# First shift and scale on TensorE, an ordered head, four landing buffers and a spread rotation in a two-layer hybrid trunk

## The chip, the cores and the metric

One core of a Trainium2 chip runs the whole kernel. The metric is the device time of one execution in microseconds (us), as the median of several. Engines are called as in the profile: PE is TensorE, DVE is VectorE, ACT is ScalarE, POOL is GpSimd, and SP is SyncE, whose queue issues most of the DMAs.

## The reference

What must be computed is a stack of two layers over 512 tokens of width 1024, conditioned on one vector c. Each layer normalises x, scales and shifts it by values computed from c (adaLN), projects it once to all inputs of two mixers (a sparse attention with an index of top keys, and a chunked state-space scan), merges the mixers by gates and adds the result to x.

```python
def _layer(x, c, w_ada, b_ada, norm_g, w_in, ...):
    mod = jax.nn.silu(c) @ w_ada + b_ada
    shift, scale, gate = jnp.split(mod, 3, axis=-1)
    h = _rmsnorm(x, norm_g) * (1.0 + scale[:, None, :]) + shift[:, None, :]
    proj = h @ w_in
    (q, k, v, g_att, qi, ki, wi, z, xbc, dt_raw, gl_att, gl_ssd) = _split_cols(proj, IN_SIZES)
    q = _rope(q.reshape(B, L, N_ATT_HEADS, HEAD_DIM), cos[:, None, :], sin[:, None, :])
    ...
    merged = jax.nn.sigmoid(gl_att) * y_att + jax.nn.sigmoid(gl_ssd) * y_ssd
    return x + gate[:, None, :] * (merged @ w_out)
```

All is float32. The kernel splits each factor of a product into a high and a low part of a shorter format and sums three products: high by high, low by high and high by low.

## The kernel before, in words

**Layout.** x lies transposed in SBUF: 128 channels on the partitions, eight channel blocks (k = 0 to 7), 512 tokens along the free dimension. `hh` and `hl` (tiles H0 and H1; in the profile both are called H) hold the high and low part of the normalised, scaled and shifted input. The modulation (adaLN) comes in 24 blocks of 128 channels per layer: 0 to 7 shift, 8 to 15 scale, 16 to 23 gate. For a block, `ada_block` (L147) multiplies a 128x1024 piece of weights by `cb`, which is silu(c) repeated on all partitions, on VectorE and accumulates along the row (L149); ScalarE adds the bias (L152 for a scale, `gsc`; L154 for a shift, `mod`).

**The head.** TensorE repeats c on all partitions by two multiplications with one row (L130), and ScalarE takes silu of it (L295). The four pairs of blocks of x are squared, one block of a pair by ScalarE (L297), the other by VectorE (L298), and added (L299). TensorE sums them over the channels with a constant (L301), 256 tokens into each of two banks. From each half comes a reciprocal root (`rstd_from`, L263 and L265 on ScalarE, two correction steps L266 and L267 on VectorE). Before the first H, blocks 8 and 0 of the modulation are needed. `make_h` (L310) builds H: a product on VectorE (L312), the high part on ScalarE (L313), the low part on VectorE (L315). `chain` (L142) fixes VectorE's order in the head, `in_row` (L288) a part of ScalarE's.

**The token projection.** `tok_section` (L365) loops over k and, within it, over two groups of weights: K (468 columns, with the index keys, the step sizes and the value) and Q (512 columns), for four token blocks each. L379, L380 and L381 are the three products, per token block one after the other. The weights come through class `W`: `load` starts a DMA of 512 KB into one of `RAWB` = 3 landing buffers `raw` (L175, on SP's queue), `split` casts the high part on ScalarE (L194) and subtracts on VectorE (L195). Modulation blocks of later use stand in the same list and land in the same buffers; so a load waits until the step that reads the buffer's former content is done. `pre0` builds H for the next k and the next two modulation blocks beside it.

**The rotations.** `rope_k` rotates the four token blocks of K: products with cosine (L435) and sine (L437) from the bank, a sum (L439), casts on ScalarE (L451, L452), low parts by subtraction on VectorE (L454, L455), transposes on TensorE (L466). `rope_q` does the same for Q (low part L489, transposes L494) and is written out in full behind it. Then come the channel blocks: `block` (L249) with products L254, L255, L256, with other generators (index scores, state-space steps, attention) interleaved by `tick`.

**What sets the order.** The kernel's text gives a program order with priorities; a scheduler makes each engine's list from it, and the order of VectorE and ScalarE in the head is fixed by hand with dependencies that carry no wait. Loads stand in one list on SP's queue.

**Later.** In the attention, L798 and L799 make scores for four heads, L801 evicts them on VectorE with the row's maximum.

## Time and profile before

| | |
|---|---|
| time, median of 3 executions | 924.76 us (922.68 to 924.89) |
| profiled execution, its own time | 926.5 us |
| its span, first to last instruction | 924.7 us |
| mean granted TensorE clock | 0.992 |
| busy: PE, DVE, ACT, POOL | 906.5, 703.9, 521.0, 49.6 us |
| chain that ended last, share of the span | PE 88%, DVE 5%, DMA 4%, ACT 1% |
| moved by DMA | 128.05 MB, 138 GB/s |

Times are microseconds from the start of the span. The busy time of TensorE counts an instruction from its start to its modelled end, and instructions overlap, so a stretch can be full of busy time and yet run at the lower clock; the granted clock stands beside it, as a share of the full one. The chain is followed back from the last instruction to what released each step.

### The profile page before, as it was taken

The numbers are of one execution on the slowest core, as the hardware profiler recorded it, in microseconds if no ns is written. First come the engines' busy times: TensorE is split into PE (matmuls) and PEld (weight loads), VectorE is DVE, ScalarE is ACT, GpSimd is POOL, SyncE is SP. The second block draws the span as 40 slices with busy tenths as digits, with TensorE's granted clock in tenths as the row PEclk, the third lists the DMA queues.
The fourth block names the chain that finished last, engine by engine and source line by source line (L and its number), as shares of the span: only waits on it lengthen the run. The fifth ranks groups of instructions, "written<-read, shape, count | busy, mean of one in ns | idle before, by whom it ended". The sixth has DMA issues, their size and how long they took to land.

```text
span 924.7 us, 13016 instructions
## 1 busy us (share of the span) xinstructions
PE 906.5 (98%) x4780; PEld 743.8 (80%) x4780; DVE 703.9 (76%) x1384; ACT 521.0 (56%) x946; POOL 49.6 (5%) x53
## 2 busy tenths in 40 slices
PE   8999999999999999999999999999999999999996
PEld 4887788888887877777998878888888878778895
DVE  7987999999775765678497699999984675455834
ACT  5457894386265754535365588745653775463433
POOL 0000110031000000000000001102210000000000
PEclk8999999999999999999999999999999999999999
DMA  9832433232346432687344225234323532334502
GB/s 357 317 114 69 164 111 103 103 137 84 102 139 200 138 133 72 220 282 266 96 134 140 89 93 180 94 98 131 125 66 117 169 117 91 92 122 149 207 24 91
DMA packets 40609, 128.05 MB, mean 138 GB/s; under 512 B 4417, under 2 KB 6721, under 8 KB 40546
## 3 DMA queue, kind: packets, MB, share of 16 engines
q1 hardware_dynamic: 36162, 111.43, 36.6%
q0 software_dynamic: 4384, 15.80, 4.9%
q8 instruction: 37, 0.61, 0.3%
q14 instruction: 26, 0.21, 0.1%
HBM read 118.76 MB, written 8.46 MB: 138 GB/s over the span
## 4 chain that ended last, share of the span: by engine, by line
PE 88%; DVE 5%; DMA 4%; ACT 1%; issue 1%; SPq 0%; DVEq 0%; ACTq 0%
PE mm L254 21%; PE mm L255 21%; PE mm L256 21%; PE av L826 2%; PE tr L821 2%; DMA raw<-ada 2%; DVE wlo L195 1%; PE qk L723 1%; PE mm L379 1%; PE mm L381 1%; PE mm L380 1%; PE qk L798 1%; PE qk L799 1%; DMA raw<-wt 1%; PE av L740 1%
## 5 line engine op out<-in xcount | busy, mean ns | idle before, releaser
L254 PE MATMUL mm<-H,whi 128*128 128x512 f32 x640 | 258.6, 404 | 0.0
L256 PE MATMUL mm<-H,wlo 128*128 128x512 f32 x640 | 251.4, 393 | 0.0
L255 PE MATMUL mm<-H,whi 128*128 128x512 f32 x640 | 251.2, 393 | 0.0
L195 DVE TENSOR_TENSOR wlo<-raw,whi 128x1024 fp32r<-128x1024 f32 (+2 forms) x130 | 158.0, 1215 | 56.6 <-ACT whi L194 54.7
L194 ACT CAST whi<-raw 128x1024 fp32r<-128x1024 f32 (+2 forms) x130 | 130.3, 1003 | 113.1 <-PE mm L255 84.7
L254 PEld LDWEIGHTS mm<-H,whi 128*128 128x128 f32 x640 | 120.6, 188 | 26.3 <-issue 3.9
L256 PEld LDWEIGHTS mm<-H,wlo 128*128 128x128 f32 x640 | 120.5, 188 | 25.6 <-issue 0.3
L255 PEld LDWEIGHTS mm<-H,whi 128*128 128x128 f32 x640 | 120.7, 189 | 24.4 <-issue 1.9
L581 DVE MAX8 m<-B 128x8 f32<-128x256 f32 (+2 forms) x96 | 53.1, 554 | 1.2
L603 DVE SCALAR_TENSOR_TENSOR tmp<-mm,prm,tmp 128x511 f32<-128x511 f32 (+2 forms) x72 | 52.8, 736 | 0.0
L582 DVE MATCH_REPLACE8 B<-m,B 128x256 f32<-128x256 f32 (+2 forms) x96 | 52.0, 541 | 0.0
L254 PE MATMUL mm<-X,whi 128*128 128x512 f32 x128 | 51.6, 403 | 0.0
L256 PE MATMUL mm<-X,wlo 128*128 128x512 f32 x128 | 50.2, 392 | 0.3 <-DVE wlo L195 0.3
L803 ACT ACTIVATE S<-S,mx 128x128 f32<-128x128 f32 (+3 forms) x64 | 35.5, 556 | 25.3 <-DVE mx L801 25.2
L149 DVE SCALAR_TENSOR_TENSOR raw<-raw,KI 128x1024 f32<-128x1024 f32 x20 | 24.5, 1223 | 31.5 <-DMA raw<-ada 31.4
L712 ACT ACTIVATE X<-X,acs 128x128 f32<-128x128 f32 x128 | 40.5, 390 | 0.1
L255 PE MATMUL mm<-G,whi 128*128 128x512 f32 x96 | 37.7, 393 | 0.2 <-DVE G L870 0.2
L254 PE MATMUL mm<-S,A 128*128 128x256 f32 x128 | 36.9, 289 | 0.0
L256 PE MATMUL mm<-S,C 128*128 128x256 f32 x128 | 36.2, 283 | 0.0
L898 DVE SCALAR_TENSOR_TENSOR X<-mm,mod,X 128x256 f32<-128x256 f32 (+1 forms) x24 | 13.7, 571 | 28.5 <-PE mm L256 28.5
L822 ACT COPY B<-tr 128x512 f32<-128x512 f32 x40 | 22.7, 583 | 20.9 <-PE tr L821 20.6
L715 POOL TENSOR_TENSOR S<-S,G 128x768 f32<-128x768 f32 x16 | 31.1, 1954 | 60.8 <-ACT G L604 31.2
(269 smaller groups left out, 1766.0 us busy)
## 6 DMA issues: line engine op xcount, KB each, us to landing
raw<-wt SPq DMA_DIRECT2D x103, 512.0 KB, 3.5
raw<-ada SPq DMA_DIRECT2D x20, 512.0 KB, 3.9
X<-AD POOLq DMA_DIRECT2D x16, 512.0 KB, 4.4
raw<-wk SPq DMA_DIRECT2D x12, 468.0 KB, 3.4
B<-ada SPq DMA_DIRECT2D x9, 512.0 KB, 4.4
raw<-wq SPq DMA_DIRECT2D x8, 512.0 KB, 3.9
gsave<-tmp SPq DMA_DIRECT2D x16, 256.0 KB, 2.4
tmp<-gsave SPq DMA_DIRECT2D x16, 256.0 KB, 4.0
```

The source lines that it names most:

```text
L149: link(dve.scalar_tensor_tensor(w, w, 1.0, cb, op0=OP.mult, op1=OP.mult, accum_out=m))
L194: act.copy(hi[:, :n], r[:, :n])
L195: link(dve.tensor_sub(lo[:, :n], r[:, :n], raw(hi[:, :n])))
L254: pe.matmul(out, h, rh[:, k, cols], start=k == 0, stop=False)
L255: pe.matmul(out, h, rl[:, k, cols], start=False, stop=False)
L256: pe.matmul(out, lw, rh[:, k, cols], start=False, stop=k == n - 1)
L581: dve.max(m8, sc)
L582: dve.match_replace(sc, m8, sc, GONE)
L603: dve.scalar_tensor_tensor(cc[:, i:], p[:, :L - i], cw(3 - i), cc[:, i:], op0=OP.mult, op1=OP.add)
L712: act.activation(ab[:, h, i], ab[:, h, i], AF.Relu, scale=-1.0, bias=acs[:, 2 * kt + h, i:i + 1])
L715: pool.tensor_tensor(cs_, cs_, BC[:, 2 + g, 128:].rearrange("p (c l) -> p c l", c=3)[:, None] .to_broadcast([128, 2, 3, 128]), op=OP.mult)
L803: act.activation(PP[:, e, :n], PP[:, e, :n], AF.Exp, bias=mx[:, e:e + 1], scale=-1.0, accum_out=sums_[:, e:e + 1])
```

## The change

1. *First shift and scale on TensorE.* A new input `cc` is c as a 128x8 column tile, loaded on ScalarE's queue into `ccol`; silu of it is the first step on ScalarE. A new input `adn` holds blocks 8 and 0 of the first layer's modulation weights in the layout that TensorE takes as weights. Behind the sums stand 16 fp32 multiplications of a 128x128 weight tile and one column (L326 of the changed kernel), eight into each of two columns of one bank `rows`, then one idle multiplication of 512 columns (L331). ScalarE reads `rows`. The two L149 steps of VectorE for these blocks go.
2. *An ordered head.* Each Square stands before the Silu of the same turn. `rstd_from` is cut into `root` and `corrected`; ScalarE's order is now fixed through both roots, scale, first cast, shift, both halves of H, second cast. VectorE does the corrections and products of both halves first, then their low parts, then the split of the first weights. In `tok_section` all high-by-high and low-by-high products of a group come first, the four products with the low weights last; for the first k the order is fixed by dependencies.
3. *Four landing buffers* (`RAWB` = 4).
4. *Rotation of queries beside the channel blocks.* `rope_q` is spawned as a generator; the index waits until it is done and takes its tile `IX` only then.

```diff
-RAWB = 3
+RAWB = 4
...
+IDLE = 1
...
+    ccol = consts.tile([128, KT], F32, name="ccol")
+    act.dma_start(ccol, cc)
...
     def load_ada(k):
-        sp.dma_start(aws[2 * k + 1], ada[0, 8 + k])
-        sp.dma_start(aws[2 * k], ada[0, k])
+        sp.dma_start(aws[2 * k + 1], adn[1] if k == 0 else ada[0, 8 + k])
+        sp.dma_start(aws[2 * k], adn[0] if k == 0 else ada[0, k])
...
+        def cast(self, i, arow):
+            self.load(i)
+            n = self.src[i][1]
+            self.his[i] = wp.tile([128, 1024], F32R, name="whi", tag="whi", bufs=WB)
+            with tc.high_priority(W_PRIO):
+                arow(act.copy(self.his[i][:, :n], self.loaded[i][:, :n]))
...
+    in_row(act.activation(ccol, ccol, AF.Silu))
     for k in range(0, KT, 2):
+        sq, sq1 = scratch(), scratch()
+        in_row(act.activation(sq, xt[:, k], AF.Square))
         if k < 4:
             in_row(act.activation(*silu[k // 2], AF.Silu))
-        sq, sq1 = scratch(), scratch()
-        in_row(act.activation(sq, xt[:, k], AF.Square))
...
+    rows = bank("mm")
+    for b in (1, 0):
+        for k in range(KT):
+            made = pe.matmul(rows[:, b:b + 1], aws[b][:, k * 128:(k + 1) * 128], ccol[:, k:k + 1],
+                             start=k == 0, stop=k == KT - 1)
+            tc.add_manual_dep(made.ins, summed.ins.name, NOSYNC)
+            summed = made
+    for i in range(IDLE):
+        made = pe.matmul(warm.rearrange("p (a b) -> p a b", a=4), ones, ones[:, None, :].to_broadcast([128, 4, 128]),
+                         start=True, stop=True)
...
-    ada_block(0, 8, cb, aws[1], chain)
-    ada_block(0, 0, cb, aws[0], chain)
...
-                        pe.matmul(acc[t][:, :n], hh[:, k, ts], a, start=k == 0, stop=False)
-                        pe.matmul(acc[t][:, :n], hh[:, k, ts], b, start=False, stop=False)
-                        pe.matmul(acc[t][:, :n], hl[:, k, ts], a, start=False, stop=k == KT - 1)
+                        for h in (hh, hl):
+                            made = pe.matmul(acc[t][:, :n], h[:, k, ts], a, start=k == 0 and h is hh, stop=False)
...
+                    for t in blocks:
+                        pe.matmul(acc[t][:, :n], hh[:, k, t * 128:(t + 1) * 128], b, start=False, stop=k == KT - 1)
...
         def pre0(k):
             if k == 0:
-                for cols, s in zip(HALVES, sums):
-                    rstd_from(rst[:, cols], s, D, True, chain)
-                    h = make_h(0, k, cols, chain)
+                sides = [(rst[:, cols], s) for cols, s in zip(HALVES, sums)]
+                ts = [root(*side, in_row) for side in sides]
+                ada_block(0, 8, None, rows[:, 1:2], arow=in_row)
+                w.cast(ids0[0], in_row)
+                ada_block(0, 0, None, rows[:, 0:1], arow=in_row)
+                hs = [make_h(0, k, cols, chain, in_row) for cols in HALVES]
+                for side, t, h in zip(sides, ts, hs):
+                    corrected(*side, t, chain)
                     next(h)
-                    if cols.start == 0:
-                        w.split(ids0[0], chain)
-                        w.load(ids0[3])
+                w.cast(ids0[1], in_row)
+                for h in hs:
                     for _ in h:
                         pass
+                w.split(ids0[0], chain)
+                w.load(ids0[3])
...
-        for _ in rope_q():
-            pass
+        spawn(rope_q(), 1)
...
-        IX = slot("B2", [128, 1152], F32)
+        IX = []
...
         def index():
+            while any(g[0].__name__ == "rope_q" for g in gens):
+                yield "wait"
+            IX.append(slot("B2", [128, 1152], F32))
```

How the lists of the engines move is shown at three places. In them `H_163` and `H_180` are `hh`, `H_164` and `H_181` are `hl`; `mm`, `qk`, `tr` and `av` are banks of PSUM, where the sums lie in `av` and `tr`, the accumulators of K in `qk` and `mm`. Lines are those of each kernel.

ScalarE in the head, from the first reciprocal root; before:

```order
7 L263 ACTIVATE rst<-av,epst 128x256
8 L152 ACTIVATE gsc_116<-mod_114,gb_118,prm 128x1
9 L265 ACTIVATE tmp<-rst 128x256
10 L263 ACTIVATE rst<-tr,epst 128x256
11 L154 ACTIVATE mod_114<-mod_114,prm 128x1
12 L194 CAST whi<-raw 128x936
13 L265 ACTIVATE tmp<-rst 128x256
14 L313 ACTIVATE H_163<-tmp,mod_114 128x256
15 L194 CAST whi<-raw 128x1024
16 L313 ACTIVATE H_163<-tmp,mod_114 128x256
```

and in the changed kernel (L276 and L278 are the roots and squares, L158 the scale, L160 the shift, L190 and L209 casts, L344 the high part of H):

```order
10 L276 ACTIVATE rst<-av,epst 128x256
11 L278 ACTIVATE tmp<-rst 128x256
12 L276 ACTIVATE rst<-tr,epst 128x256
13 L278 ACTIVATE tmp<-rst 128x256
14 L158 ACTIVATE gsc_118<-mm,gb_120,prm 128x1
15 L190 CAST whi<-raw 128x936
16 L160 ACTIVATE mod_116<-mm,prm 128x1
17 L344 ACTIVATE H_180<-tmp,mod_116 128x256 x2
18 L190 CAST whi<-raw 128x1024
```

The scale, which stood behind the first root and read VectorE's sum (`mod`), now stands behind both roots and reads TensorE's bank; both halves of H stand before the second cast.

VectorE at the end of the token projection, where the accumulators of K are rotated, from the cosine product of token block 1; before (L435 cosine, L437 sine, L439 sum, L454 and L455 subtractions, L449 step sizes, L195 the split of channel weights):

```order
66 L435 TENSOR_TENSOR tmp<-qk,B_165 128x384
67 L454 TENSOR_TENSOR B_498<-tmp,B_498 128x4x64
68 L455 TENSOR_TENSOR B_498<-tmp,B_498 128x2x128
69 L437 TENSOR_TENSOR tmp<-qk,B_165 128x6x32 x2
70 L449 TENSOR_TENSOR dtr<-mm,prm 128x16
71 L439 TENSOR_TENSOR tmp<-tmp 128x384
72 L435 TENSOR_TENSOR tmp<-mm,B_165 128x384
73 L454 TENSOR_TENSOR B_498<-tmp,B_498 128x4x64
74 L437 TENSOR_TENSOR tmp<-mm,B_165 128x6x32 x2
75 L195 TENSOR_TENSOR wlo<-raw,whi 128x1024
76 L455 TENSOR_TENSOR B_498<-tmp,B_498 128x2x128
```

and in the changed kernel (L478, L480, L482, L497, L498, L492 and L210 are the same in that order):

```order
63 L478 TENSOR_TENSOR tmp<-qk,B_182 128x384
64 L497 TENSOR_TENSOR B_517<-tmp,B_517 128x4x64
65 L498 TENSOR_TENSOR B_517<-tmp,B_517 128x2x128
66 L480 TENSOR_TENSOR tmp<-qk,B_182 128x6x32 x2
67 L492 TENSOR_TENSOR dtr<-mm,prm 128x16
68 L482 TENSOR_TENSOR tmp<-tmp 128x384
69 L210 TENSOR_TENSOR wlo<-raw,whi 128x1024
70 L497 TENSOR_TENSOR B_517<-tmp,B_517 128x4x64
71 L498 TENSOR_TENSOR B_517<-tmp,B_517 128x2x128
72 L478 TENSOR_TENSOR tmp<-mm,B_182 128x384
73 L480 TENSOR_TENSOR tmp<-mm,B_182 128x6x32 x2
```

The split of the third channel weights, which stood behind the subtraction L454 of block 1 and the cosine and sine products of block 2, now stands ahead of all of them.

VectorE ahead of the first eviction of attention scores (L801, L846 in the changed kernel), where modulation blocks (L149, now L152) and splits (L195, now L210) are worked off; before:

```order
364 L149 SCALAR_TENSOR_TENSOR raw,mod_114<-raw,KI 128x1024
365 L195 TENSOR_TENSOR wlo<-raw,whi 128x1024
366 L764 SCALAR_TENSOR_TENSOR tmp<-C,prm,tmp 128x512 x3
367 L766 TENSOR_TENSOR D_2438<-tmp,X 128x512 x3
368 L195 TENSOR_TENSOR wlo<-raw,whi 128x1024
369 L764 SCALAR_TENSOR_TENSOR tmp<-C,prm,tmp 128x512
370 L149 SCALAR_TENSOR_TENSOR raw,mod_114<-raw,KI 128x1024
371 L766 TENSOR_TENSOR D_2438<-tmp,X 128x512
372 L195 TENSOR_TENSOR wlo<-raw,whi 128x1024
373 L149 SCALAR_TENSOR_TENSOR raw,mod_114<-raw,KI 128x1024
374 L801 ISA S,mx<-ctab,qk 128x128
```

and in the changed kernel:

```order
363 L210 TENSOR_TENSOR wlo<-raw,whi 128x1024
364 L152 SCALAR_TENSOR_TENSOR raw,mod_116<-raw,KI 128x1024
365 L809 SCALAR_TENSOR_TENSOR tmp<-C,prm,tmp 128x512 x3
366 L811 TENSOR_TENSOR D_2459<-tmp,X 128x512 x3
367 L210 TENSOR_TENSOR wlo<-raw,whi 128x1024
368 L809 SCALAR_TENSOR_TENSOR tmp<-C,prm,tmp 128x512
369 L152 SCALAR_TENSOR_TENSOR raw,mod_116<-raw,KI 128x1024
370 L811 TENSOR_TENSOR D_2459<-tmp,X 128x512
371 L210 TENSOR_TENSOR wlo<-raw,whi 128x1024
372 L152 SCALAR_TENSOR_TENSOR raw,mod_116<-raw,KI 128x1024
373 L846 ISA S,mx<-ctab,qk 128x128
```

The first two rows have changed places; from the products L764 (now L809) on, the rows are the same in both, down to split, modulation block, eviction.

On TensorE, all 12 transposes of the first two token blocks (`turn_k`) stand ahead of the first channel block in the changed kernel, and eight of them before.

## Rows read from the trace of the kernel before

**Rows 1.** Page, first part: span, and each engine's busy us.

```profile
span 924.7 us, 13016 instructions
...
PE 906.5 (98%) x4780; PEld 743.8 (80%) x4780; DVE 703.9 (76%) x1384; ACT 521.0 (56%) x946; POOL 49.6 (5%) x53
```

**Rows 2.** View of waits, TensorE: total us, times, longest us.

```profile
PE qk L379 <- ACT H L313: 2.8, 1, 2.8
PE qk L798 <- DVE mx L801: 2.3, 2, 2.0
```

**Rows 3.** Timeline of TensorE, head: start us, us, engine line operation, [idle before].

```profile
12.92 0.59 PE L301 MATMUL tr<-tmp,mones 128*128 128x256 f32 x2
16.35 0.76 PE L379 MATMUL qk<-whi,H 128*128 128x468 f32 x1 [2.83 <-ACT H L313]
...
24.73 0.37 PE L379 MATMUL qk<-whi,H 128*128 128x468 f32 x1
```

**Rows 4.** View of stretches: busy us (instructions) per engine, PEclk, DMA share, GB/s.

```profile
16.00:22.90 6.90, 6.55 (x16) 4.89 (x16) 6.25 (x12) 3.19 (x6) 0.00 (x0) 0.51 1.03 412
285.70:289.10 3.40, 3.40 (x10) 2.62 (x9) 2.35 (x7) 2.39 (x6) 0.00 (x0) 0.50 0.33 128
```

**Rows 5.** Timeline of VectorE and the DMA queue, 275 to 283 us.

```profile
276.17 1.22 DVE L149 SCALAR_TENSOR_TENSOR raw<-raw,KI 128x1024 f32<-128x1024 f32 x1
...
277.42 0.33 SPq L175 DMA_DIRECT2D raw<-ada  x1
...
282.84 1.23 DVE L149 SCALAR_TENSOR_TENSOR raw<-raw,KI 128x1024 f32<-128x1024 f32 x1 [2.91 <-DMA raw<-ada]
```

**Rows 6.** Timeline of VectorE, head.

```profile
11.72 1.22 DVE L149 SCALAR_TENSOR_TENSOR C<-C,G 128x1024 f32<-128x1024 f32 x1
...
15.13 0.48 DVE L312 SCALAR_TENSOR_TENSOR tmp<-X,gsc,rst 128x256 f32<-128x256 f32 x1
15.61 1.13 DVE L195 TENSOR_TENSOR wlo<-raw,whi 128x936 fp32r<-128x936 f32 x1
...
22.87 0.75 DVE L312 SCALAR_TENSOR_TENSOR tmp<-X,gsc,rst 128x512 f32<-128x512 f32 x1
```

**Rows 7.** Timeline of ScalarE, head.

```profile
13.49 0.38 ACT L152 ACTIVATE gsc<-mod,gb,prm 128x1 f32<-128x1 f32 x1
...
14.62 0.96 ACT L194 CAST whi<-raw 128x936 fp32r<-128x936 f32 x1
...
15.80 0.50 ACT L313 ACTIVATE H<-tmp,mod 128x256 fp32r<-128x256 f32 x1
...
23.71 0.73 ACT L313 ACTIVATE H<-tmp,mod 128x512 fp32r<-128x512 f32 x1 [1.56 <-DVE tmp L312]
```

**Rows 8.** Timeline of TensorE, last Q multiplications and first channel block.

```profile
62.46 0.46 PE L466 MATMUL qk<-identr,B 128*128 128x128 f32 x4
63.33 0.51 PE L466 MATMUL qk<-identr,B 128*128 128x128 f32 x4 [0.41 <-DVE B L454]
63.87 0.47 PE L254 MATMUL mm<-H,whi 128*128 128x512 f32 x1
```

**Rows 9.** Timeline of TensorE's weight loads, an fp32 sum near the end.

```profile
915.88 0.30 PEld L907 LDWEIGHTS av<-tmp,mones 128*128 128x128 f32 x2 [1.00 <-ACT tmp L906]
```

**Rows 10.** Timeline of VectorE, end of the projection.

```profile
62.21 0.55 DVE L435 TENSOR_TENSOR tmp<-mm,B 128x384 f32<-128x384 f32 x1
62.76 0.42 DVE L454 TENSOR_TENSOR B<-tmp,B 128x256 fp32r<-128x256 f32 x1
63.11 0.61 DVE L437 TENSOR_TENSOR tmp<-mm,B 128x192 f32<-128x192 f32 x2
63.74 1.22 DVE L195 TENSOR_TENSOR wlo<-raw,whi 128x1024 fp32r<-128x1024 f32 x1
```

**Rows 11.** Timeline of ScalarE, end of the projection.

```profile
62.66 1.05 ACT L194 CAST whi<-raw 128x1024 fp32r<-128x1024 f32 x1
```

**Rows 12.** View of waits, VectorE; columns as in rows 2.

```profile
DVE raw L149 <- DMA raw<-ada: 31.4, 15, 5.3
```

More of the change, by code (lines that the diff above doesn't have):

```diff
@@ L62, in trunk @@
 @with_exitstack
-def trunk(ctx, tc, x, c, wk, wq, wt, wa, ada, pk, cst, out):
+def trunk(ctx, tc, x, c, cc, wk, wq, wt, wa, ada, adn, pk, cst, out):
     nc = tc.nc
@@ L113, in trunk @@
     identr = consts.tile([128, 128], F32R, name="identr")
-    dve.tensor_copy(identr, idt[:, :128])
+    tail = [dve.tensor_copy(identr, idt[:, :128])]
     ident = raw(identr)
@@ L139, in trunk @@
     gb = [consts.tile([128, KT], F32, name=f"gb{l}") for l in range(DEPTH)]
-    tail = []
     def chain(ins):
@@ L145, in chain, with ada_block @@
         tail.append(ins)
-    def ada_block(l, b, cb, w, link=lambda ins: None):
+    def ada_block(l, b, cb, w, link=lambda ins: None, arow=lambda ins: None):
         m = mods[l][:, b:b + 1]
-        link(dve.scalar_tensor_tensor(w, w, 1.0, cb, op0=OP.mult, op1=OP.mult, accum_out=m))
+        if cb is not None:
+            link(dve.scalar_tensor_tensor(w, w, 1.0, cb, op0=OP.mult, op1=OP.mult, accum_out=m))
+            row = m
+        else:
+            row = w
         if 8 <= b < 16:
             j = b - 8
-            act.activation(gsc[l][:, j:j + 1], m, AF.Identity, scale=par(l, P_NG + j), bias=gb[l][:, j:j + 1])
+            arow(act.activation(gsc[l][:, j:j + 1], row, AF.Identity, scale=par(l, P_NG + j), bias=gb[l][:, j:j + 1]))
         else:
-            act.activation(m, m, AF.Identity, bias=par(l, P_BA + b))
+            arow(act.activation(m, row, AF.Identity, bias=par(l, P_BA + b)))
     class W:
@@ L300, in trunk @@
         for cols, s in zip(HALVES, sums):
-            pe.matmul(s, mones, sq[:, cols], start=k == 0, stop=k == KT - 2)
+            summed = pe.matmul(s, mones, sq[:, cols], start=k == 0, stop=k == KT - 2)
+    rows = bank("mm")
[8 more added lines that the diff above has]
+                         start=True, stop=True)
+        tc.add_manual_dep(made.ins, summed.ins.name, NOSYNC)
+        summed = made
     pool.dma_start(cbs[:], cb[:1])
@@ L363, in trunk, with tok_section @@
         accK = [bank(t) for t in BK.split()]
-        def tok_section(parts, blocks, pre):
+        def tok_section(parts, blocks, pre, row=None):
             got = {}
@@ L410, in trunk @@
             accQ = [bank(t) for t in BQ.split()]
-            rest = tok_section([(ids_k[0], NKS, accK, 0), (ids_q, 512, accQ, LAG)], range(NB), pre0)
+            rest = tok_section([(ids_k[0], NKS, accK, 0), (ids_q, 512, accQ, LAG)], range(NB), pre0, [])
             for _ in range(KT):
@@ L552, in view @@
         def view(b):
-            return IX[:, place[b]:place[b] + 128 * (b + 1)]
+            return IX[0][:, place[b]:place[b] + 128 * (b + 1)]
         def scores(b):
@@ L988, in _layout @@
     return {
-        "x": con(rows(f["x"][0].T).transpose(1, 0, 2)), "c": con(f["c"]),
+        "x": con(rows(f["x"][0].T).transpose(1, 0, 2)), "c": con(f["c"]), "cc": con(f["c"].reshape(KT, 128).T),
         "wk": con(np.stack(wks)), "wq": con(np.stack(wqs)), "wt": con(np.stack(wts)), "wa": con(np.stack(was)),
-        "ada": con(np.stack(adas)), "pk": pk, "cst": cst,
+        "ada": con(np.stack(adas)),
+        "adn": con(np.stack([rows(f["w_ada"][0][:, b * 128:b * 128 + 128]).transpose(1, 0, 2).reshape(128, 1024)
+                             for b in (0, 8)])), "pk": pk, "cst": cst,
     }
```

30 lines of the change are left out of this document (20 added, 10 removed).

## The prediction

> **What bounds the kernel now.** I read the first part of the page first: TensorE (PE) is busy 906.5 of 924.7 us [rows 1]. A change can win only where TensorE stands or runs at its lower clock, and it loses wherever it makes TensorE stand. So I read TensorE's waits next. Two are long: 2.8 us for the first normalised input H in the head, and 2.3 us for the first eviction of attention scores, L801 [rows 2]. The timeline of the head shows the first. TensorE has its last sum of squares behind it at 13.5, begins the input projection at 16.35, and from there to the second k step at 24.73 no wait is recorded [rows 2, 3]. But the clock: from 16.0 to 22.9 the granted clock is 0.51, its lower level of 1.2 GHz, with TensorE busy 6.55 us [rows 4]. At 2.4 GHz that work takes half, so the head loses 3.3 us to the clock beside the 2.8. The fall follows a stand of 2.8 us.
>
> The second place shows the same thing once more. VectorE (DVE) stands 2.91 us at L149 until 282.84 for the landing of an adaLN block, and L801 is queued right behind it [rows 5]. TensorE waits, and from 285.7 to 289.1 it is busy 3.40 us at 0.50 [rows 4]: 1.7 us lost. The place costs 2.3 + 1.7 = 4.0 us.
>
> The profiled execution took 926.5 us, 1.7 above the median of 924.76. I sum changes against the profiled one and put the sum on the median.
>
> **The first scale and shift.** Removed: two multiply-and-accumulate steps of 1.22 us on VectorE [rows 6]. They stand beside the last sums, and ScalarE (ACT) has the scale at 13.49, just when the sums end [rows 7]: in the kernel before they cost nearly nothing. Added on TensorE, behind the last sum: 16 fp32 multiplications with one column each, two passes each, so 32 weight loads. No row shows a one-column multiplication. From the nearest rows, four 128-column transposes, each with a weight load, take 0.46, or 0.115 each [rows 8], and two passes' fp32 weight loads take 0.30, or 0.15 each [rows 9]. That is 3.7 to 4.8 us; I take 3.7, since the transposes too run back to back. They start when the last sum is issued, about 13.3 [rows 3], perhaps 0.2 earlier, since the first Square now stands before the first Silu. Both columns lie in one bank, and the scale's step on ScalarE waits for the last of the 16: R = 16.8.
>
> What follows R on ScalarE is in the order shown: scale 0.38, cast 0.96, shift, two H steps of 0.50 [rows 7]. With the next step starting 0.1 before an end, the first H is done at R + 1.9, and the projection starts at 18.7, against 16.35. That is not yet the loss, because the second k step is held by VectorE. Its queue after R: two products of 0.48 (which wait for the scale), two low parts of H of as much, the split of the K weights 1.13, two L149 of 1.22, the split of the Q weights 1.22, the product of the next step 0.75 [rows 6, 10]. The second low part waits for the second H (R + 2.4) and ends at R + 2.9. The rest sums to 5.5, and H of the next step adds 0.73 [rows 7]: R + 9.1, less some 0.4 for overlaps, or 25.5. Now it is 24.73, so **+0.8** if TensorE keeps its clock.
>
> If it does not, TensorE itself holds the second step. Its 8.4 us from 16.35 to 24.73 less 3.3 for the clock are 5.1 for 23 multiplications, 5.3 for the 24 that stand there now. Begun at 18.7 and at half pace to 22.9 as today, 2.1 are done and 3.2 remain: 26.1, **+1.4**. In both cases one multiplication more lies behind (0.2). I take **+1.0**. The ends: all 32 passes at half pace, twice 3.7, put R at 20.5 and the loss at +4; a full clock from earlier on, so that sums and rows end 2 us earlier, gives -1.0. The idle multiplication is not waited for by the scale. The small load of the condition column on ScalarE's queue lands beside the first rows of x, which VectorE waits for anyway: nothing.
>
> **The K tail.** In the projection the four multiplications with the low weight parts now stand last in each step. While every step follows another that costs nothing. It shows at the end, where the accumulators are rotated. Now the last Q multiplication hands over at 62.46, four transposes follow, four more at 63.33 after a short wait, and the first channel block starts at 63.87, 1.4 later [rows 8]. VectorE got there by running the subtraction L454 of block 1 at 62.76, the sine products of block 2 at 63.11, and only then the 1.22 us split of the third channel weights at 63.74 [rows 10]. In the new order that split stands ahead of the subtraction and of the cosine and sine products; and TensorE has all 12 transposes ahead of the first channel block, which itself takes a bank that the sine products free. The split waits for a 1.05 us cast [rows 11], and that for the last multiplication with the high part, some 0.9 before the end. Counted from the end of Q: cast done +0.45, split to +1.6, the two subtractions (0.42 each) to +2.4, cosine 0.55 and sine 0.61 to +3.4 [rows 10]. TensorE starts the block at +3.4 instead of +1.4, with four transposes more done (0.4): **+1.6**. Ends: 0.8 if TensorE's end of Q comes later against VectorE than now, 2.2 if each step also loses a hand-over of 0.1.
>
> **Four landing buffers.** The wait that costs something is the one at 282.84. Its load is issued at 277.42, at the end of the L149 that began at 276.17 [rows 5]. In the new order the last three VectorE rows before the eviction are the same (split, L149, eviction), and the load of that L149 is still issued only when the L149 before it is done. The other 14 of the 15 waits of this kind, 31.4 us in all, are VectorE's own, with no wait of TensorE beside them [rows 2, 12]. I take **0**; the other end is -4.0.
>
> **Rotation of queries.** The rotation is spread between channel blocks rather than written out before them. TensorE records no long wait behind it now [rows 2], the engines' lists were interleaved there already, and only the index scores wait for its end. 0, with 0.5 either way.
>
> **Sum:** 1.0 + 1.6 + 0 = +2.6, so 929.1 for a profiled execution and **927.4** for the median. Measurement of this kernel can tell about 0.3%, 2.8 us, from no change; so the forecast lies at the upper edge of "the same" (922.0 to 927.5).
>
> **Rivals.**
>
> (a) *The clock falls behind the K tail.* In the new order there is a stretch of 3.4 us, from the last Q multiplication to the first channel block, with 12 transposes (1.4 us) and about 2 us of standing. A stand of 2.0 at 284 was followed by 3.4 us at half clock [rows 2, 4], and the present stretch of 1.4 us was followed by none. If it falls, the price is the 1.7 of the place at 285: +4.3, or **929.1**, slower. [...] The Trainium skill ("TensorE: Matmul & The Clock Gate", Part 4: PE-mode transpose) has it that transposes do not count as busy in the same way for the clock; by that rule the whole 3.4 us would be idle, and this rival the likelier. The rows do not contradict it, and none here shows transposes alone for so long. I give it 0.27.
>
> (b) *The fourth buffer ends the stand at 282.* With one adaLN block more in flight the load would be issued one L149 earlier. For it: that is what the wait is for. Against it: the order of issue. -4.0 + 2.6 = -1.4, **923.4**, no slower; 0.16.
>
> (c) *The head gains.* The clock rises before the sums end, or the row multiplications are shorter than a weight load: -1.0 + 1.6, **925.4**; 0.11.
>
> (d) *Both (b) and (c), the K tail at its low end:* -4.0 - 1.0 + 0.8, **920.6**, faster; 0.10.
>
> (e) *Row multiplications at half pace,* the rest as forecast: +4 + 1.6, **930.4**; 0.06.
>
> **How the numbers follow.** The forecast has 0.30, with a range of its own of 925.5 to 929 (ends of the two terms nearest to their values). The range 921 to 931 leaves out most of (d) and the tails of (a) and (e). Faster by over 0.3% is (d) and a little of (b) and (c): 0.14. Slower is (a), (e) and the upper part of the forecast: 0.43. The rest, 0.43, is within 0.3%.
>
> **What would show it.** Right: TensorE's wait for H ends near 18.7, the second k step starts near 25.5 to 26, the first channel block 3.4 us after the last Q multiplication, and the waits list still has L846 (now the eviction's line) behind an adaLN load near 284. Wrong: row multiplications ending before 16 or after 19; a channel block that follows Q within 2 us; no adaLN wait ahead of the first eviction. Rival (a) shows as a granted clock near 0.5 for some us after the channel blocks start.

## The result, and the profile after

| | before | changed |
|---|---|---|
| time, median (range) | 924.83 us (922.68 to 925.56) | 932.88 us (931.58 to 934.22) |
| ratio | 1 | 1.0082, 95% interval 1.0061 to 1.0104 |
| profiled execution, its own time | 926.5 us | 931.58 us |
| its span | 924.7 us | 929.8 us |

The changed kernel is slower by 8.1 us at the median, 5.5 more than the forecast and above its range. The two profiled executions lie only 5.1 apart, since that of before lies above its kernel's range and that of the changed one is its quickest; a second profile of each (experiments 15 and 16) has spans of 930.4 and 922.8, 7.6 apart. Both pairs are used below.

The page's first part and TensorE's waits in the changed kernel, in the manner of [rows 1, 2]:

```profile
span 929.8 us, 13091 instructions
...
PE 911.0 (98%) x4814; PEld 749.6 (81%) x4814; DVE 701.2 (75%) x1380; ACT 522.4 (56%) x948; POOL 49.4 (5%) x53
```

```profile
PE qk L843 <- DVE mx L846: 4.3, 3, 1.8
PE qk L509 <- DVE B L497: 1.6, 1, 1.6
...
PE mm L269 <- DVE tmp L645: 0.7, 1, 0.7
```

VectorE has 2.7 us less work and TensorE 4.5 us more. The wait for the first H is gone from the top, because the row multiplications and the idle one now fill it (in the second profile, experiment 15, 1.0 of it is left). In its place stand waits for L846 (4.3, where 2.3 stood), for the rotated K (L497), and for L645, an eviction on VectorE for which the trace of before has no wait.

**Where the time went.** Compare the start of the same TensorE instruction in two traces: the K transposes, the first channel block, then later channel blocks, named by their time in the first profile of before. The table gives how late (us) the changed kernel is.

| place | 62.5 | 64 | 116 | 143 | 398 | 448 | 723 | 738 | end |
|---|---|---|---|---|---|---|---|---|---|
| first profiles | 1.7 | 3.6 | 4.7 | 5.7 | 3.8 | 1.5 | 2.2 | 5.2 | 5.0 |
| second profiles | 0.8 | 2.7 | 2.2 | 6.2 | 4.8 | 4.5 | 5.3 | 7.7 | 7.6 |

Four steps stand out: the head (to 62.5), the K tail (62.5 to 64, the same 1.9 in both), a place between 116 and 143, and one between 723 and 738, in the second layer. The first profile of before lost 2.0 between 398 and 448 that its second one did not; this is why the upper row falls there.

**The head.** TensorE's timeline, in the manner of [rows 3]:

```profile
12.89 0.60 PE L322 MATMUL tr<-tmp,mones 128*128 128x256 f32 x2
13.33 4.12 PE L326 MATMUL mm<-ccol,C 128*128 128x1 f32 x32
17.31 2.05 PE L331 MATMUL mm<-ones 128*128 128x512 f32 x2
19.45 2.21 PE L411 MATMUL qk<-whi,H 128*128 128x468 f32 x4
...
26.74 0.69 PE L411 MATMUL qk<-whi,H 128*128 128x468 f32 x2
```

The 32 passes took 4.12, or 0.129 each, and ended at 17.45, the R of the prediction. The idle multiplication filled nearly all the time to the first H, at half pace. The second k step begins at 26.74, against 24.73. What held it is on ScalarE and VectorE, in the manner of [rows 6, 7]:

```profile
17.48 0.35 ACT L158 ACTIVATE gsc<-mm,gb,prm 128x1 f32<-128x1 f32 x1 [2.66 <-PE mm L326]
...
17.87 0.49 DVE L343 SCALAR_TENSOR_TENSOR tmp<-X,gsc,rst 128x256 f32<-128x256 f32 x1 [2.93 <-ACT gsc L158]
18.27 0.42 DVE L282 SCALAR_TENSOR_TENSOR tmp<-tr,tmp 128x256 f32<-128x256 f32 x1
...
18.72 0.42 DVE L283 SCALAR_TENSOR_TENSOR rst<-tmp,rst 128x256 f32<-128x256 f32 x1
18.89 0.51 ACT L344 ACTIVATE H<-tmp,mod 128x256 fp32r<-128x256 f32 x1
19.18 0.48 DVE L343 SCALAR_TENSOR_TENSOR tmp<-X,gsc,rst 128x256 f32<-128x256 f32 x1
...
25.96 0.73 ACT L344 ACTIVATE H<-tmp,mod 128x512 fp32r<-128x512 f32 x1 [1.57 <-DVE tmp L343]
```

The two corrections of the second half (L282, L283) are ready early, but they stand behind the first product, which waits for the scale. H of the second step is done at 26.69, and TensorE begins at 26.74; its own row of multiplications ends there too, so in this execution both limits coincide. In the second profile they do not: there the rows take 3.63 and end at 15.75, the projection begins at 17.75, H of the second step is done at 24.99, and TensorE, at a clock of 0.50 from 19.4 to 22.9, begins that step only at 26.14.

The view of stretches, columns as in [rows 4], shows the clock of the head, and then that of the K tail:

```profile
13.00:16.00 3.00, 3.00 (x28) 2.95 (x26) 0.85 (x2) 1.67 (x4) 0.00 (x0) 1.00 1.03 415
16.00:19.40 3.40, 3.36 (x11) 1.78 (x10) 1.46 (x4) 1.88 (x4) 0.00 (x0) 0.54 1.02 404
...
66.00:69.00 3.00, 2.34 (x12) 1.94 (x13) 2.94 (x10) 1.85 (x5) 0.00 (x0) 0.75 0.57 175
69.00:72.00 3.00, 3.00 (x16) 2.42 (x15) 2.60 (x8) 0.74 (x2) 0.00 (x0) 0.68 0.00 0
```

**The K tail.** TensorE and VectorE from the last Q multiplications, in the manner of [rows 8, 10]:

```profile
64.18 0.46 PE L509 MATMUL qk<-identr,B 128*128 128x128 f32 x4
64.56 1.23 DVE L210 TENSOR_TENSOR wlo<-raw,whi 128x1024 fp32r<-128x1024 f32 x1 [0.20 <-ACT whi L209]
...
65.70 0.42 DVE L497 TENSOR_TENSOR B<-tmp,B 128x256 fp32r<-128x256 f32 x1
...
66.27 0.85 PE L509 MATMUL qk<-identr,B 128*128 128x128 f32 x8 [1.63 <-DVE B L497]
...
66.84 0.61 DVE L480 TENSOR_TENSOR tmp<-mm,B 128x192 f32<-128x192 f32 x2
...
67.51 0.80 PE L269 MATMUL mm<-H,whi 128*128 128x512 f32 x1 [0.39 <-DVE tmp L480]
```

The split of 1.23 stands ahead of the subtraction, and the channel block begins 67.51 - 64.18 = 3.33 after the end of Q, where it was 1.41.

**The second layer.** Around 732, the DMA queue, VectorE and TensorE:

```profile
730.09 2.14 SPq L658 DMA_DIRECT2D gsave<-tmp  x2
...
732.67 0.33 SPq L182 DMA_DIRECT2D raw<-ada  x1
...
733.98 0.08 DVE L846 DVE_READ_ACCUMULATOR2_ANT mx<- 128x1 f32 x1
...
738.39 1.23 DVE L152 SCALAR_TENSOR_TENSOR raw<-raw,KI 128x1024 f32<-128x1024 f32 x1 [4.33 <-DMA raw<-ada]
...
739.54 0.28 DVE L846 CUSTOM_DVE_ANT_0 S<-ctab,qk 128x128 f32<-128x128 f32 x1
...
739.88 0.33 PE L843 MATMUL qk<-KK,A 128*128 128x128 f32 x1 [1.65 <-DVE mx L846]
...
742.82 0.33 PE L843 MATMUL qk<-KK,A 128*128 128x128 f32 x1 [0.84 <-DVE mx L846]
```

Two evictions are done, and then VectorE stands 4.33 us at a modulation block, with the next evictions queued behind it. It is the third block that lands in the second layer. In the kernel before, the second block stands ahead of the first eviction; the load of the third is issued only at 737.12, and its step comes behind the four evictions of each of two groups:

```profile
729.88 1.23 DVE L149 SCALAR_TENSOR_TENSOR raw<-raw,KI 128x1024 f32<-128x1024 f32 x1 [2.17 <-DMA raw<-ada]
...
732.17 0.28 DVE L801 CUSTOM_DVE_ANT_0 S<-ctab,qk 128x128 f32<-128x128 f32 x1
...
737.12 0.33 SPq L175 DMA_DIRECT2D raw<-ada  x1
...
738.28 0.29 DVE L801 CUSTOM_DVE_ANT_0 S<-ctab,qk 128x128 f32<-128x128 f32 x1
...
740.57 1.23 DVE L149 SCALAR_TENSOR_TENSOR raw<-raw,KI 128x1024 f32<-128x1024 f32 x1 [0.38 <-DMA raw<-ada]
```

So the fourth buffer brings both forward: the load by 4.5 us, and its step from behind the evictions to a place between them, where the load has not landed yet.

### The profile page after: what moved, and what is told of

Read it like the earlier page. It is cut to its first block, busy times and chain, and to the rows that moved or that the text cites. A ratio compares the mean times of both kernels' runs of the same rounds, so it can differ in the third digit from the quotient of the medians.

```text
span 929.8 us, 13091 instructions
## 1 busy us (share of the span) xinstructions
PE 911.0 (98%) x4814; PEld 749.6 (81%) x4814; DVE 701.2 (75%) x1380; ACT 522.4 (56%) x948; POOL 49.4 (5%) x53
## 4 chain that ended last, share of the span: by engine, by line
PE 85%; DVE 8%; DMA 2%; ACT 2%; issue 1%; DVEq 0%; ACTq 0%
PE mm L269 20%; PE mm L270 20%; PE mm L271 20%; PE mm L411 2%; DVE wlo L210 2%; PE av L871 2%; DMA raw<-ada 2%; PE tr L866 2%; PE qk L411 2%; PE tr L411 2%; DVE B L624 1%; PE qk L768 1%; PE mm L418 1%; DVE tmp L645 1%; DVE m L623 1%
## 5 line engine op out<-in xcount | busy, mean ns | idle before, releaser
L210 DVE TENSOR_TENSOR wlo<-raw,whi 128x1024 fp32r<-128x1024 f32 (+2 forms) x130 | 157.5, 1211 | 61.2 <-ACT whi L209 60.9
L209 ACT CAST whi<-raw 128x1024 fp32r<-128x1024 f32 (+2 forms) x128 | 128.5, 1004 | 114.7 <-PE mm L270 85.7
L645 DVE SCALAR_TENSOR_TENSOR tmp<-mm,prm,tmp 128x509 f32<-128x509 f32 (+2 forms) x72 | 52.8, 738 | 0.0
L152 DVE SCALAR_TENSOR_TENSOR raw<-raw,KI 128x1024 f32<-128x1024 f32 x20 | 24.4, 1222 | 22.5 <-DMA raw<-ada 22.5
```

The lines of the kernel that those rows point to most:

```text
L209: act.copy(hi[:, :n], r[:, :n])
L210: link(dve.tensor_sub(lo[:, :n], r[:, :n], raw(hi[:, :n])))
L645: dve.scalar_tensor_tensor(cc[:, i:], p[:, :L - i], cw(3 - i), cc[:, i:], op0=OP.mult, op1=OP.add)
```

## The experiments

Ratios are to the kernel before, with their 95% intervals. Each is to executions of before that were measured beside it, so that a difference of two medians and the difference of their ratios can disagree by about 1 us. "Less" and "above" go by medians, against the first measurement of the changed kernel; its second (experiment 15) is 0.9 lower. "Late" is against the first profile of before, as in the table.

**1. Three buffers again.**

```diff
-RAWB = 4
+RAWB = 3
```

> The changed kernel with three landing buffers again. Theory (buffers): with four buffers an adaLN step stands between the evictions of layer 1 and its load is issued late; with three it stands ahead of them. The two waits of TensorE for L846 near 738 and 742 (2.5 us together, as recorded) go, the one near 287 stays, and the 2.3 us that the changed kernel won between 385 and 431 us is given back in part. Net 0.5 to 2.9 us faster than the changed kernel. Rival (phase): the waits near 738 come from the later start of everything and not from the buffers; then they stay and the time stays within 0.5 us.

929.34 us, 1.0043 (1.0028 to 1.0058): 3.5 less. The lateness does not grow in the second layer (2.5 at 448, 2.9 at 738): the stop there belongs to the buffers. The waits for L645 near 127 and 145 are larger, 2.8.

**2. Products by token block again,** for all k but the first.

```diff
+                    if k:
+                        for t in blocks:
+                            ...
+                            pe.matmul(acc[t][:, :n], hh[:, k, ts], a, start=False, stop=False)
+                            pe.matmul(acc[t][:, :n], hh[:, k, ts], b, start=False, stop=False)
+                            pe.matmul(acc[t][:, :n], hl[:, k, ts], a, start=False, stop=k == KT - 1)
+                        continue
```

> The changed kernel, where for every k but the first the three products stand together per token block as before. Theory (K tail): the order of VectorE at the end of the projection goes back to that of before, the first channel block starts about 1.4 us after the last Q multiplication instead of 3.3, the granted clock stays 1.0 behind it: 3 to 4 us faster than the changed kernel. Rival (head): the tail is late because the head is late, so the channel block still starts 3 us after Q: under 0.5 us of gain.

927.63 us, 1.0029 (1.0017 to 1.0041): 5.2 less. The channel block follows Q after 1.4 and the clock stays at 1.00. The whole lateness of 2.0 at the channel block was there at the K transposes. Another 1.4 comes between 143 and 186. The stop in the second layer stays.

**3. Rotation of queries in full.**

```diff
-        spawn(rope_q(), 1)
+        for _ in rope_q():
+            pass
```

> The changed kernel with the rotation of queries written out in full ahead of the channel blocks. Theory: the engines' lists interleave it in either case, so the time stays within 1 us of the changed kernel. Rival: the generator holds back the index and with it the later stages, and the time falls by 1 to 3 us.

931.62 us, 1.0065 (1.0049 to 1.0081): 1.3 less, and the intervals overlap. The waits for L645 shrink to 0.3, and the clock stays at 1.00 behind the K tail.

**4. The head of before** (two L149 on VectorE, no rows, the old order of the head).

```diff
-    rows = bank("mm")
...
+    ada_block(0, 8, cb, aws[1], chain)
+    ada_block(0, 0, cb, aws[0], chain)
```

> The changed kernel with the head of before: scale and shift of blocks 8 and 0 on VectorE, no multiplications with the condition column, no idle one, ScalarE's and VectorE's order of before; products with the low weights still last, four buffers, rotation spread. Theory (head): the second k step starts near 24.7 instead of 26.7, and the gain of 1.5 to 2 us lasts to the end. Rival: later waits swallow it, and the time stays within 0.5 us of the changed kernel.

927.66 us, 1.0025 (1.0013 to 1.0037): 5.2 less (3.5 by the ratio against that of experiment 15), though the new head by itself is late by less than 2. The parts don't simply add.

**5. Before with four buffers.**

```diff
-RAWB = 3
+RAWB = 4
```

> The kernel before with four landing buffers and nothing else. Theory (buffers): an adaLN step now stands between the evictions of layer 1 here too, with its load issued late; two waits of TensorE near 733 to 738 appear, about 2.9 us together with what follows, and the wait near 284 stays: about 928.0. Rival (buffers also win): all runs with four buffers, and less clearly the one with three, were 2 us better than before between 385 and 431 us; if four buffers bring that, the waits of before there (0.5 at 410, 1.3 at 429) go and the time is about 926.

925.86 us, 1.0009 (0.9998 to 1.002). The stop in the second layer appears (late -3.2 at 723, -0.4 at 738: 2.8), the one at 284 stays, though the clock holds behind it, and nothing is late between 398 and 448, as in the second profile of before. TensorE's waits:

```profile
PE qk L798 <- DVE mx L801: 5.3, 4, 2.4
```

**6. Changed with three buffers and products by block,** the edits of 1 and 2: the head and the rotation are left.

```diff
-RAWB = 4
+RAWB = 3
...
+                    if k:
```

> The changed kernel with three buffers and the products by block: what remains is the head with TensorE's columns and the spread rotation. Theory (parts add): 927.6 of the run with products by block, less the 2.9 us of the waits in layer 1: about 924.7, with the head's 2 us still in it. Rival (parts overlap): head and buffers were counted twice and the time stays near 927.

925.24 us, 0.9996 (0.9985 to 1.0007). The trace is 1.0 late at the K transposes and 1.8 at 186, and 1.2 early at its end. So here the new head shows in the trace, not in the time. (Against the second profile of before, which lacks the loss between 398 and 448, the trace is 0.7 late at its end.)

**7. Rotation alone on before** (the first k keeps the changed kernel's order of products).

```diff
-        for _ in rope_q():
-            pass
+        spawn(rope_q(), 1)
```

> The kernel before with the spread rotation and nothing else of the change (old head, products by block, three buffers). Theory: the head's 2 us go as well, about 922.7, if the 2 us between 385 and 431 us come from the spread rotation. Rival: they were a feature of the one profiled execution of the kernel before, which took 1.7 us more than its median; then the time is that of before, 925 within 1 us.

926.34 us, 1.0 (0.9984 to 1.0016): no change, within 1.5 us.

**8. Before with the modulation blocks one item later:** one place in the list of layer 0 stays empty, and all later blocks move back by one.

```diff
-            if late and (l == 0 or nadd[0] % 2 == 0):
+            if late and (nadd[0] not in (3,) if l == 0 else nadd[0] % 2 == 0):
```

> The kernel before, with one thing changed that the change does not touch: in the list of layer 0 no adaLN block follows the third item, so that all later blocks come one item later. The last VectorE rows ahead of the first eviction are then adaLN, split, eviction rather than split, adaLN, eviction, and the load of that block is issued two rows earlier. Theory (the wait near 284 is one late load, and the fall of the clock its consequence): TensorE's wait shrinks from 2.2 to under 1 us, the granted clock stays 1.0, and the time falls by 2.5 to 4 us, to 921 to 922.6. Rival: the load lands as late, or another stands in its place: 924.5 to 925.5.

928.59 us, 1.0039 (1.0026 to 1.0052). The theory missed. The stand at 284 goes (late -0.3 at 274, -3.5 at 288), but another block, at 286, takes the place ahead of evictions (late -0.4 at 320); TensorE waits 1.22 for an eviction before 364.08, 0.84 before 384.24 and 1.5 near 431, and the trace is 2.3 late at 398. VectorE at 286, where the eviction L801 comes only at 288.64:

```profile
286.35 1.23 DVE L149 SCALAR_TENSOR_TENSOR raw<-raw,KI 128x1024 f32<-128x1024 f32 x1 [1.86 <-DMA raw<-ada]
```

**9. Four idle multiplications in the K tail** of the changed kernel, ahead of the second group of transposes; the order of the transposes around them is fixed.

```diff
+                for _ in range(4 if l == 0 and t == 1 and g == 0 else 0):
+                    made = pe.matmul(raw(p).rearrange("p (a b) -> p a b", a=4), ones, ...,
+                                     start=True, stop=True)
```

> The changed kernel, where TensorE works off four idle multiplications of 512 columns (two passes each, some 1.8 us at full clock) into the bank of the next transposes while it waits in the K tail. Theory (clock): the wait of 1.6 us there is filled, the granted clock stays 1.0 from 66 to 72 us, and the time falls by 1.2 to 2 us against the changed kernel, although not one useful instruction is earlier. Rival: the fall has no part in the loss, later waits take it up; the time stays within 0.5 us, or grows by what the idle multiplications hold up (0.3 us).

931.18 us, 1.007 (1.0055 to 1.0086). The stretches behind the tail hold the clock:

```profile
64.00:67.00 3.00, 3.00 (x9) 1.28 (x7) 3.00 (x9) 0.96 (x4) 0.00 (x0) 1.00 0.27 81
67.00:70.00 3.00, 3.00 (x24) 2.69 (x23) 2.93 (x9) 2.61 (x8) 0.00 (x0) 1.00 0.23 94
```

But the channel block comes 3.0 later against the K transposes, not 1.9, and at 116 the 2.9 that are left of it equal what the tail with the lower clock costs. Up to there, keeping the clock this way gained nothing; the time is 1.7 below the first median of the changed kernel and 0.8 below its second, with intervals that overlap.

**10. Low-weight products last, alone on before.**

```diff
+                    if k:
+                        ...
+                        for t in blocks:
+                            pe.matmul(acc[t][:, :n], hh[:, k, t * 128:(t + 1) * 128], b, start=False, stop=k == KT - 1)
+                        continue
```

> The kernel before, with nothing changed but the products: for every k but the first the four with the low weights stand last. Theory (K tail): the first channel block starts 3.3 us after the last Q multiplication and the clock falls behind it, and part of it is taken up later: 1.5 to 3.9 us slower than before, 926.5 to 929. Rival (the loss needs the late head): without the late head the tail has slack, and the time is within 0.5 us of before.

927.7 us, 1.0031 (1.0016 to 1.0047). Late -0.5 at the K transposes, 1.4 at the channel block, 2.5 at 71: the tail costs 1.9, and the lower clock behind it (0.57 from 67 to 70) 1.1 more.

**11. Modulation blocks behind the evictions,** three buffers, on before. In the attention a modulation step is held back until a group's four evictions are written out, and follows the last of them by a dependency without a wait.

```diff
+        def follow(self, ins):
+            if self.after is not None:
+                tc.add_manual_dep(ins.ins, self.after.ins.name, NOSYNC)
...
-                self.split(j)
+                if self.src[j][2] is not None and self.after is not None and j < self.late and j not in self.ready:
+                    self.held.append(j)
+                else:
+                    self.split(j)
...
-                            dve.tensor_tensor_reduce(PP[:, e, :n], bias, p, -0.125, -GONE, OP.add, OP.min,
+                            w.after = dve.tensor_tensor_reduce(PP[:, e, :n], bias, p, -0.125, -GONE, OP.add, OP.min,
...
+                    unhold()
```

> The kernel before, with one rule more that the change does not have: an adaLN step that would come while attention runs is given out behind the fourth eviction of a group (by a dependency without a wait), not ahead of it. Three buffers. Theory (evictions queue behind a late load): the wait near 284 and its half clock go, about 3 to 4 us faster than before: 921 to 922. Rival: as in the run where the blocks came one item later, the steps find other places to collide, and the time is 924 to 928.

922.08 us, 0.9972 (0.996 to 0.9983). Late 0.8 at 274 and -3.1 at 320: in these two traces 3.9 of the 4.0 that the prediction read from [rows 2, 4] are won. By the ratio it is 2.6, and one reason lies in the traces: in 1, 4, 5 and 10 TensorE waits 2.0 to 3.1 near 284 as well, but its clock stays at 1.00 behind the wait, so that the 1.7 of the clock is not lost in every execution.

**12. The same with four buffers.**

```diff
-RAWB = 3
+RAWB = 4
```

> The same rule with four buffers. If the load's start is what counts, the fourth buffer lets it start one step earlier and the time is 0.5 to 1.5 us below that with three. If, as the run of before with four buffers has it, a fourth buffer moves steps and starts no load earlier, both agree within 0.5 us.

919.93 us, 0.9947 (0.9933 to 0.9962): the quickest, 0.5% ahead of before and 2.2 below 11, more than was expected. Of the 2.0 between the two traces, 1.0 is there at the K transposes already, where the traces with the head of before range from -0.9 to 0.8. The waits of TensorE have no eviction L815 (L801 of before) among the first, and VectorE runs the modulation blocks behind the evictions:

```profile
PE qk L393 <- ACT H L327: 2.9, 1, 2.9
PE mm L125 <- DVE ones L110: 1.1, 1, 1.1
PE tr L754 <- PE av L756: 0.9, 2, 0.4
```

```profile
287.51 0.29 DVE L815 CUSTOM_DVE_ANT_0 S<-ctab,qk 128x128 f32<-128x128 f32 x1
...
287.73 1.22 DVE L149 SCALAR_TENSOR_TENSOR raw<-raw,KI 128x1024 f32<-128x1024 f32 x1
```

**13. The new head alone on 12.**

```diff
-    ada_block(0, 8, cb, aws[1], chain)
-    ada_block(0, 0, cb, aws[0], chain)
+    rows = bank("mm")
```

> The kernel of run e12 with the new head alone (columns by TensorE, ordered head; products by block except in the first k, rotation in full). Theory (the head has a price of its own): the second k step starts 1.6 us later in the mean, as in the traces so far, and nothing later takes it up: 921.0 to 922.0 against 919.9. Rival (the head costs only with other waits behind it): 919.5 to 920.4.

921.65 us, 0.9952 (0.9934 to 0.9971), 1.7 above 12 at the median and 1.8 at the end of the trace; by the ratios it is only 0.5 us.

**14. Low-weight products last, alone on 12,** the edit of 10.

```diff
+                        for t in blocks:
+                            pe.matmul(acc[t][:, :n], hh[:, k, t * 128:(t + 1) * 128], b, start=False, stop=k == KT - 1)
```

> The kernel of run e12 with products last alone. Theory (VectorE is late from the K tail on, whatever the clock does): all traces with products last and the rotation of before stand 2.8 to 3.0 us later near 116 us than at the end of Q, so 922.5 to 923. Rival (part is taken up by the stage after 116 us): 920.5 to 921.5.

921.88 us, 0.9956 (0.9939 to 0.9973), 2.0 above 12 (0.8 by the ratios), between the two expected ranges. The channel block is 1.9 late and the clock stays at 1.00.

**15 and 16. The changed kernel and the kernel before once more,** without an edit, for a second profile of each.

> The changed kernel once more. If the spread between executions is the clock's phase, its first projection starts between 18 and 19.5 us and the time lies between 930 and 934, median near 932.5; if the four executions so far were slow by chance, 930 to 931.

> The kernel before once more. If its one profile was slow by chance (1.7 us above its median), the waits near 410 and 429 are shorter here and the second k step starts up to 1 us earlier, at a time near 925; if they belong to the kernel, they stand here too.

931.99 us, 1.0063 (1.004 to 1.0085), and 924.76 us, 0.9996 (0.9978 to 1.0014). The changed kernel's first projection begins at 17.75, ahead of the expected 18 to 19.5. In the kernel before, the waits near 410 and 429 are gone. The changed kernel's waits, and VectorE ahead of one of them:

```profile
PE qk L843 <- DVE mx L846: 4.4, 3, 2.5
PE mm L269 <- DVE tmp L645: 3.2, 3, 1.5
```

```profile
125.38 0.56 DVE L623 MAX8 m<-B 128x8 f32<-128x384 f32 x1
125.86 0.73 DVE L645 SCALAR_TENSOR_TENSOR tmp<-mm,prm,tmp 128x511 f32<-128x511 f32 x1
...
126.58 0.54 DVE L624 MATCH_REPLACE8 B<-m,B 128x384 f32<-128x384 f32 x1
127.04 0.74 DVE L645 SCALAR_TENSOR_TENSOR tmp<-mm,prm,tmp 128x510 f32<-128x510 f32 x1
127.69 0.55 DVE L623 MAX8 m<-B 128x8 f32<-128x384 f32 x1
128.16 0.73 DVE L645 SCALAR_TENSOR_TENSOR tmp<-mm,prm,tmp 128x509 f32<-128x509 f32 x1
```

TensorE waits 1.49 for the last of these. The three steps that free its bank are interleaved with the search for the largest index scores (MAX8, MATCH_REPLACE8), and VectorE does not stand in these rows: it is simply behind.

## Why the prediction was wrong, point by point

**The head, forecast +1.0.** The mechanism was right and two terms were small. R came at 17.45, not 16.8: the passes took 0.129 each, inside the forecast 0.115 to 0.15, but above the value taken. Five of the eight traces with the new head have 3.63 us for the 32 (the 3.7 of the forecast); in this one, and in experiments 2 and 3, the clock had fallen and they took 4.12 to 4.77. The first H was done at 19.40, R + 1.95, as forecast. The step that failed is "Its queue after R: two products of 0.48 ... two low parts of H": it left out the two corrections of the second half between the products. The second low part ends at R + 3.3, not R + 2.9; the rest took 6.0, against 5.8. The eight traces with the new head begin the K transposes 0.5 to 2.0 later than the first profile of before, 1.2 in the mean; the ten with the old head -0.9 to +0.8, in the mean -0.2. That is +1.4, and 13 against 12 gives 1.7, or 0.5 by the ratios. In three of the eight traces, the changed kernel's second among them, the rows end before 16, which the prediction had as a sign of being wrong; there (second step at 26.14) the other limit that it named holds, TensorE at half pace, which it had put at 26.1. That the two removed L149 were worth nothing was right.

**The K tail, forecast +1.6.** Right in its mechanism and close in size. The channel block starts 3.33 after Q (forecast 3.4) and is 1.9 later in all seven traces with the low weights last and no filling. Where the clock holds, 0.5 of that comes back by 116, which is the 0.4 of the transposes done early: +1.4.

**Rival (a), the clock behind the K tail,** came in four of those seven traces (the changed kernel's first, 1, 4, 10) and not in 3, 14 and the changed kernel's second. Where it fell, lateness grows by 0.9 to 1.1 by 116 instead of shrinking by 0.5: 1.5, against the forecast 1.7. So it was not one case or the other, but something that differs between executions. By the Trainium skill ("TensorE: Matmul & The Clock Gate", Part 4: PE-mode transpose), as the prediction used it, the stretch counts as idle; the rows agree in those four traces, and in the other three about the same stretch had no such consequence. Where it fell, not all of the loss reached the end: in 1, 4 and 10 the clock then stays at 1.00 behind the wait near 284, where it falls in both traces of before and both of the changed kernel, and 1.2 to 1.4 come back between 274 and 320.

**Four landing buffers, forecast 0.** This is the step that failed most: "The wait that costs something is the one at 282.84". That wait indeed stays (TensorE's gap before 288.9, the clock at 0.56 behind it), and rival (b) fell, but not because loads start no earlier: counted in order, the block ahead of the first eviction is the fourth of its layer in before (load at 277.42) and the fifth with four buffers (experiment 5: load at 277.41, where before issues it at 284.10). Each load starts a step earlier, and the next block takes the place. The prediction took equal rows for the same blocks, and it took into account only the wait that the trace of before showed. In the second layer the same shift by one entry puts a modulation block between the second and third eviction; its load is issued at 732.67, 4.5 earlier than before, and VectorE still stands for it until 738.39. It costs 2.3 to 3.0 in each trace with four buffers and the order of the lists as it was (the changed kernel's two, 2, 3, 4, 5, 9) and nothing in those with three. The term was about +2.8 at this place, where the prediction gave 0 to -4.0 and no bound on the side of a loss. Three buffers again give the changed kernel back 3.5 (experiment 1), but by its ratio experiment 5 pays only 0.8: with four buffers its trace also lacks the 2.0 between 398 and 448, which some traces with three buffers have and others lack.

**Rotation, forecast 0.** Right by itself as far as 1.5 us can tell (experiment 7: 1.0, 0.9984 to 1.0016).

**What had no term.** The terms of single parts are 1.4 (head), 1.4 to 2.9 (tail), and 0.8 to 2.8 (buffers). Between 116 and 143 the changed kernel loses 1.0 more in one trace and 4.0 in the other, of which 0.7 and 3.2 are recorded waits for L645; experiment 1 has 2.8 there. These three traces have the head, the product order and the spread rotation together. In the traces with one of the three undone the wait is 0.3 or nothing (2, 3, 4, 6, 7, 10, 13, 14), though 2, 6 and 13 lose 0.5 to 1.4 between 143 and 186 instead; with the filling of experiment 9 it does not show either. Since the changed kernel's own two traces differ by 2.5, one trace of each does not show that it takes all three. Nor do the times settle how much the parts cost together: single parts sum to 5.4 us (experiment 5: 0.8, 7: 0, 10: 2.9, 13 against 12: 1.7), or 2.1 with the low values for tail and head (14 and 13 against 12 by the ratios), and the whole is 8.1 in the first measurement and 5.8 by the ratio of the second, each with an interval of 1 to 2 us on either side. Taking out one of four gives back 3.5, 5.2, 1.3 and 5.2, or 0.9 less each against the second measurement. The second profiles add up: 0.8 (head) + 1.9 (tail) - 0.5 + 4.0 (116 to 143) - 1.4 (143 to 398) - 0.3 + 0.8 + 2.4 (second layer) - 0.1 = 7.6. That the delay of the first parts is what pushes VectorE's fixed list behind at 127 is argued from these waits and not shown; no run delays VectorE alone, and how far the rest is this or a difference of executions stays open.

**The forecast as a whole** failed by adding its parts: +2.6 for the sum, when the two terms that it had give 2.8 to 4.3, a loss of 0.8 (by time) to 2.8 (in the traces) stood at 0, and a further 1.0 and 4.0 between 116 and 143, of open cause, had no term.

## What to carry to other kernels

Work that is taken off an engine under cover buys nothing; ask instead what now stands behind the new wait, in every layer, and look through the planned order for a step that waits for a load ahead of an eviction. One more landing buffer is first of all another order: in the traces 2.8 us were lost where a step moved ahead of evictions before its load had landed (0.8 by the time of experiment 5), and with the blocks held behind the evictions four buffers were 2.2 us quicker than three (experiments 11 and 12). When two planned orders show the same rows, check that they are the same items. Parts that each make an engine a little late may meet a tight list later on; a sum of single terms says nothing of that.

## What the hardware showed that I had not expected

Sixteen one-column multiplications, back to back, did not always hold the clock: in the changed kernel's first profile TensorE was busy for 6.36 of the 6.40 us from 13 to 19.4, and its granted clock was 1.00 to 16 and 0.54 after (experiment 3: 0.81 from 13 to 16, 0.50 after). In five of the eight traces with the rows it held through them and fell only behind, where TensorE stands 1.0 us for the first H. The same kernel also starts its head differently from one execution to the next: the rows begin at 12.12 in the changed kernel's second profile, at 13.33 in its first. And the outcome of one stand differs: behind a tail of 12 transposes with 2 us of standing the clock fell in four traces of seven, and behind 2.0 to 3.1 us of waits near 284 it stayed at 1.00 in four traces (1, 4, 5, 10).
